# A decoder layer on one core: the stretch from the last output tiles to the feed-forward operands with four engines' instructions in a written order

## The chip, the cores and the metric

One core of a Trainium2 chip runs the whole kernel. Its matmul engine (TensorE, PE in the rows, with PEld for its weight loads), VectorE (DVE), ScalarE (ACT) and GpSimd (POOL) each take instructions from a queue of their own, in order; transfers between memory and the chip are issued on SyncE's queue (SP). The metric is the device time of one execution in microseconds (us), lower is better; the kernel before takes 1395.91 us.

## The reference

One decoder layer on 1024 tokens of width 1024, in float32:

```
h    = rms_norm(x, norm_mix);  proj = h @ w_in
mix  = concat(sparse_attention(proj), gated_recurrence(proj))     # 512 + 512 columns
x    = x + mix @ w_out
h    = rms_norm(x, norm_ffn)                                      # x * rsqrt(mean(x*x) + eps) * norm_ffn
gate, up = split(h @ w_gate_up)                                   # 2816 columns each
x    = x + (silu(gate) * up) @ w_down
```

The change lies where `x + mix @ w_out` and its norm turn into the operands of `h @ w_gate_up`.

## The kernel before

A float32 product is made of three matmuls in a faster format: each factor is split into a high half (an ACT copy that rounds, L111) and a low half (a DVE subtraction, L112), and `mm3` (L117 to L120) adds high x high, high x low and low x high. So the third matmul of each group of three needs the low half of the weights. `product` (L710) splits one weight tile of 128x512 into a tile `wop` and runs `mm3` four times: twelve matmuls of 512 columns.

Tokens come in eight tiles of 128. Attention runs tile by tile; when a tile is done, `nsa_out(t, n)` (L733) multiplies its mixed values with half n of the output weights, adds the result to `x1[:, t]` (L497), and after n = 1 stores the row block to memory (L738) and forms the second norm: an ACT square with a running sum (L242), a reciprocal root on 128x1 numbers by twelve small DVE steps (`rsqrt`, L122 to L131), a scaling on ACT (L745) and the gain `g_bc` on POOL (L746); the tiles from 4 on also have tile t-4 subtracted from their first half (L748). The last tile (t = 7) takes gain and root in one DVE instruction (L743) from a gain page loaded late, `g_last`.

The feed-forward product uses a Strassen-like scheme with 2x2 blocks, so its operands are blocks of `x1` and of sums and differences of them. `operand(op, src, t, bank)` (L720) makes one block of an operand: four PE transposes into a PSUM bank (L724; the tag "s" has four banks), an ACT copy of the high half (L727) and a DVE subtraction for the low half (L728). `b11` is made during attention. The others are b21 and t2o (in `opA`, which takes the place of attention's probabilities `pbig`), b22 and t1o (in `opB`), t3o and t4o (in `opC`): 24 blocks. `pair_a(t)` makes b22 and t1o of tile t+4; `pair_d(t)` makes three differences of tiles t and t+4 on POOL (L987 to L989, the first on DVE for t = 3); `pair_b(t)` makes t2o, t3o and t4o from them. `gate_up_a(f)` loads the weights of feed-forward tile f in four parts and runs its products with b11 and b21. For f = 0 and 1 the b11 products (`first`) have weights loaded into the free `qtok` pages and run at the end of attention. `gate_up_s1` forms weight sums on POOL (L972, L973), from which the first product on opB takes its weights.

What sets the order: the kernel's text gives a priority, and a planner with a model of instruction times orders each engine's queue ahead of the run; waits between engines are semaphores. Tiles with one tag share its buffers in turn (`rpage`: three pages of 128x1024). Pools that end give their memory to the next one; attention's pools `at` (with `g_bc` and the weight tiles) and `gpool` (with `qtok`) lie where `ff` (with `opC`, the differences "d" in six buffers, and the weight pages `epage`) comes later. The PSUM pool "pairs" of attention has to end before "banks" begins (`single_banks`).

Of the kernel before, what the change touches and what calls it, by code (L numbers as in the profile page):

```python
# [8 lines left out]
F32 = mybir.dt.float32  # L9
# [39 lines left out]
def hybrid_layer(ctx: ExitStack, tc: tile.TileContext, x, x_t, par, w_in, k_norm, pos_k, pos_v,  # L49
# [87 lines left out]
    V.tensor_copy(identb, ident)  # L137
    par_t = const.tile([P, 18], F32, name="par_t")
# [97 lines left out]
    def split_of(f):  # L236
        return lambda i: parts_of(f(i))

# [471 lines left out]

    def product(src, op, w=None, o=None):
        o = bank8() if o is None else o
        w = wring.tile([P, 2, 512], F32R, name="wop", tag="w") if w is None else w
        split(w[:, 0], w[:, 1], src)
        for c in range(4):
            sl = slice(c * P, (c + 1) * P)
            mm3(o, w[:, 0, sl], w[:, 1, sl], op[:, 0, c], op[:, 1, c], c == 0, c == 3)
        return o
# [11 lines left out]
    with tc.tile_pool(name="at", bufs=1) as at:  # L730
        g_bc = at.tile([P, D], F32, name="g_bc")
        nc.sync.dma_start(g_bc, norm_ffn[0:1, :].broadcast_to([P, D]))
        def nsa_out(t, n):  # L733
            if n == 0:
                mixed[t] = mix_parts(qtok[:, t].rearrange("p (c n) -> p c n", c=4))
            out_tile(w_t, t, n, *mixed[t], bank_f)
            if n == 1:
                nc.sync.dma_start(x1_d[t * P:(t + 1) * P, :], x1[:, t, :])  # L738
                rs2 = norm_stats(x1[:, t, :], rpage())
                if t == NT - 1:  # L740
                    g_last = rpage()
                    nc.sync.dma_start(g_last, norm_ffn[0:1, :].broadcast_to([P, D]))
                    V.scalar_tensor_tensor(x1[:, t, :], x1[:, t, :], rs2, g_last, op0=OP.mult, op1=OP.mult)  # L743
                    return
# [153 lines left out]
        for i, u in enumerate(units + [None]):  # L898
# [34 lines left out]
            if i == len(units) - NFIRST:  # L933

                for f in range(2):
                    gu_load(qtok[:, f], FS[f], 0, 0)
        first = [product(qtok[:, f], b11, at.tile([P, 2, 512], F32R, name="wop0", tag="q", bufs=3), ps_t())
                 for f in range(2)]
        for t in nq:
            nsa_out(*t)  # L940
    p12.close()
# [3 lines left out]
    single_banks()  # L945
    opA = big.tile([P, 2, 2, 4, 512], F32R, name="opA", tag="A2")
# [3 lines left out]
    b21, t2o, b22, t1o, t3o, t4o = (opA[:, 0], opA[:, 1], opB[:, 0], opB[:, 1], opC[:, 0], opC[:, 1])  # L950
# [3 lines left out]
    def gate_up_a(f):  # L954

        a = {}
        for j in range(2):
# [4 lines left out]
        return a, first.pop(0) if first else product(a[0, 0], b11), product(a[0, 1], b21, o=acc() if f < 2 else None)  # L962
# [15 lines left out]
    def pair_a(t):  # L978
        operand(b22, x1[:, t + 4, 512:1024], t, bank_s)
        if t == 3:  # L980
            V.tensor_tensor(x1[:, 7, 0:512], x1[:, 7, 0:512], x1[:, 3, 0:512], op=OP.subtract)
        operand(t1o, x1[:, t + 4, 0:512], t, bank_s)

    def pair_d(t):
        xa, xb = x1[:, t, :], x1[:, t + 4, :]
        d = dif[t] = [ff.tile([P, 512], F32, name=f"d{i}", tag="d", bufs=6) for i in range(3)]
        (G if t < 3 else V).tensor_tensor(d[0], xb[:, 512:1024], xb[:, 0:512], op=OP.subtract)  # L987
        G.tensor_tensor(d[1], d[0], xa[:, 0:512], op=OP.subtract)
        G.tensor_tensor(d[2], xa[:, 512:1024], d[0], op=OP.subtract)  # L989

    def pair_b(t):
        for i, op in enumerate((t2o, t3o, t4o)):
            operand(op, dif[t][i], t, bank_s)

    for t in range(4):
        operand(b21, x1[:, t, 512:1024], t, bank_s)
    nxt = [gate_up_a(0), gate_up_a(1)]
    for t in range(3):
        pair_a(t)
    for t in range(3):  # L1000
        pair_d(t)
        pair_b(t)
    s1s = [gate_up_s1(0, nxt[0][0])]
    pair_a(3)
    pair_d(3)
    pair_b(3)
    tmp = big.tile([P, 16, 512], F32, name="tmp", tag="A1")
# [290 lines left out]
```

## Time and profile before

| | us |
|---|---|
| three runs | 1395.39, 1395.91, 1396.53 |
| median | 1395.91 |
| the profiled execution | 1396.95 |
| its span, first to last instruction | 1395.2 |
| mean granted clock of TensorE | 0.997 of full speed |

The profiled execution is one more run, and all rows below are from it. Times in the rows count from the start of its span. Busy times of PE contain the latency of its pipeline: matmuls overlap, so what a matmul costs is the distance of two starts. An engine's idle time in square brackets is that before the instruction, with what ended it.

### The profile page before, as it was taken

How to read it: one execution, taken by the hardware profiler on the slowest of the kernel's cores; microseconds unless marked ns; L12 is line 12 of the kernel's file. 1: busy time of each engine (PE TensorE's matmuls, PEld its weight loads, DVE VectorE, ACT ScalarE, POOL GpSimd, SP SyncE). 2: the span in 40 equal slices, each digit the busy share in tenths (PEclk: the TensorE clock that was granted, in tenths of full speed). 3: DMA queues.
4: the chain of work that ended last, by engine and by line, in shares of the span. 5: the costliest groups of instructions: out<-in, count | busy, mean ns of one | idle time of the engine just before them, and what ended most of it. 6: DMA issues, size and time to landing. Idle time of an engine off the chain costs nothing.

```text
span 1395.2 us, 19645 instructions
## 1 busy us (share of the span) xinstructions
PE 1366.1 (98%) x7092; PEld 1127.8 (81%) x7092; DVE 1034.3 (74%) x1937; ACT 596.7 (43%) x1153; POOL 322.2 (23%) x297
## 2 busy tenths in 40 slices
PE   9999999999999999999998999999999999999998
PEld 7888888989977777777776788888888888888887
DVE  5317888626688887888867888888888887578764
ACT  7323333323446666566664433333333333444432
POOL 0001111011035443344345533323323320000000
PEclk9999999999999999999999999999999999999999
DMA  8411110111220001000003233333233336998521
GB/s 326 128 46 31 31 31 29 54 31 46 76 106 1 1 1 61 31 16 16 31 17 106 70 112 99 113 114 113 92 113 98 114 98 234 335 327 317 180 94 53
DMA packets 108768, 135.71 MB, mean 97 GB/s; under 512 B 6112, under 2 KB 63872, under 8 KB 108672
## 3 DMA queue, kind: packets, MB, share of 16 engines
q1 hardware_dynamic: 108672, 134.46, 28.6%
q8 instruction: 56, 0.92, 0.3%
q14 instruction: 40, 0.33, 0.1%
HBM read 105.87 MB, written 28.57 MB: 96 GB/s over the span
## 4 chain that ended last, share of the span: by engine, by line
PE 85%; DVE 10%; ACT 2%; issue 1%; POOL 1%; DMA 0%; ACTq 0%; POOLq 0%; DVEq 0%
PE bank L118 9%; PE bank L119 9%; PE bank L120 9%; PE a L118 8%; PE a L120 8%; PE a L119 8%; PE ps_t L120 4%; PE ps_t L119 4%; PE ps_t L118 4%; PE ps_t L861 3%; PE a L865 2%; PE a L866 2%; PE ps_t L375 1%; PE ps_s L839 1%; DVE nm L847 1%
## 5 line engine op out<-in xcount | busy, mean ns | idle before, releaser
L111 ACT ACTIVATE wop<-rpage 128x512 fp32r<-128x512 f32 x132 | 82.7, 630 | 156.8 <-PE bank L120 70.6
L850 POOL TENSOR_SCALAR pbig<-pbig,den,gates 128x640 f32<-128x640 f32 (+7 forms) x128 | 104.0, 817 | 167.0 <-DVE den L849 147.0
L112 DVE TENSOR_TENSOR wop<-rpage,wop 128x512 fp32r<-128x512 f32 x132 | 101.4, 771 | 13.4 <-ACT wop L111 11.3
L864 DVE TENSOR_TENSOR ph<-ps_t,ph 128x512 fp32r<-128x512 f32 x126 | 84.4, 684 | 18.5 <-ACT ph L863 17.6
L863 ACT ACTIVATE ph<-ps_t 128x512 fp32r<-128x512 f32 x126 | 72.7, 595 | 49.6 <-PE ps_t L861 38.7
L861 PE MATMUL ps_t<-ident,pbig 128*128 128x128 f32 x504 | 78.7, 275 | 2.1 <-POOL pbig L850 2.1
L381 POOL TENSOR_TENSOR kp<-kp,fp 128x256 f32<-128x256 f32 x28 | 20.3, 726 | 231.8 <-PE bank L358 180.3
L861 PEld LDWEIGHTS ps_t<-ident,pbig 128*128 128x128 f32 x504 | 61.0, 141 | 11.9 <-POOL pbig L850 3.2
L112 DVE TENSOR_TENSOR wlo<-wraw,whi 128x1024 fp32r<-128x1024 f32 (+2 forms) x27 | 32.0, 1188 | 46.2 <-PE a L120 19.3
L848 ACT ACTIVATE pbig<-ps_s,nm 128x640 f32<-128x640 f32 (+3 forms) x64 | 55.9, 875 | 24.1 <-DVE nm L847 19.0
L118 PE MATMUL bank<-wop 128*128 128x512 f32 x165 | 64.2, 389 | 0.0
L119 PE MATMUL bank<-wop 128*128 128x512 f32 x165 | 64.2, 389 | 0.0
L120 PE MATMUL bank<-wop 128*128 128x512 f32 x165 | 64.2, 389 | 0.0
L1012 POOL TENSOR_TENSOR tmp<-tmp,rpage 128x512 f32<-128x512 f32 x21 | 31.2, 1488 | 139.2 <-DVE wop L112 139.2
L111 ACT ACTIVATE wop<-act_a 128x512 fp32r<-128x512 f32 x48 | 30.3, 631 | 73.8 <-PE bank L120 48.3
L847 DVE TENSOR_REDUCE nm<-ps_s 128x1 f32<-128x640 f32 (+3 forms) x64 | 58.1, 914 | 4.7 <-PE ps_s L842 3.0
L865 PE MATMUL a<-ph,kv 128*128 128x512 f32 x132 | 58.8, 446 | 2.3 <-ACT ph L863 1.6
L866 PE MATMUL a<-ph,kv 128*128 128x512 f32 x132 | 57.5, 435 | 2.9 <-DVE ph L864 2.4
L112 DVE TENSOR_TENSOR wop<-tmp,wop 128x512 fp32r<-128x512 f32 x42 | 43.7, 1039 | 20.6 <-ACT wop L111 19.7
L111 ACT ACTIVATE wop<-tmp 128x512 fp32r<-128x512 f32 x42 | 26.6, 634 | 70.1 <-POOL tmp L1012 37.5
L112 DVE TENSOR_TENSOR wop<-act_a,wop 128x512 fp32r<-128x512 f32 x48 | 33.2, 691 | 30.7 <-ACT wop L111 30.6
L118 PE MATMUL a<-whi,hT_h 128*128 128x256 f32 (+2 forms) x168 | 55.2, 328 | 0.0
(458 smaller groups left out, 4352.3 us busy)
## 6 DMA issues: line engine op xcount, KB each, us to landing
rpage<-in_w_gate_up_dram SPq DMA_DIRECT2D x86, 256.0 KB, 3.1
raws<-in_w_down_dram SPq DMA_DIRECT2D x35, 512.0 KB, 7.5
act_a<-act_d SPq DMA_DIRECT2D x12, 1024.0 KB, 6.1
act_d<-as SPq DMA_DIRECT2D x33, 256.0 KB, 2.2
act_e<-act_d SPq DMA_DIRECT2D x6, 1024.0 KB, 8.2
act_d<-tmp SPq DMA_DIRECT2D x22, 256.0 KB, 2.2
act_d<-th SPq DMA_DIRECT2D x22, 256.0 KB, 2.1
xn<-in_x_dram SPq DMA_DIRECT2D x8, 512.0 KB, 6.0
```

The lines of the kernel that those rows point to most:

```text
L111: A.activation(hi, src, AF.Copy)
L112: V.tensor_tensor(lo, src, hi.bitcast(F32), op=OP.subtract)
L118: PE.matmul(o, ah, bh, start=first, stop=False, skip_group_check=chained)
L119: PE.matmul(o, ah, bl, start=False, stop=False, skip_group_check=chained)
L120: PE.matmul(o, al, bh, start=False, stop=last, skip_group_check=chained)
L847: V.tensor_reduce(nm, sv, axis=AX.XY, op=OP.max, negate=True)
L850: G.tensor_scalar(pp, pp, den, gates[:, qb, h * 3 + 1 + b:h * 3 + 2 + b], op0=OP.mult, op1=OP.mult)
L861: PE.transpose(pt[:, r * P:(r + 1) * P], wts[r][:, c0:c0 + P], ident)
L863: A.activation(ph[:, 0], pt, AF.Copy)
L864: V.tensor_tensor(ph[:, 1], pt, ph[:, 0].bitcast(F32), op=OP.subtract)
L865: PE.matmul(o, vst[b][:, kb, g, :], ph[:, 0], start=b == 0 and kb == kb0, stop=False)
L866: PE.matmul(o, vst[b][:, kb, g, :], ph[:, 1], start=False, stop=False)
```

## The change

All four engines get a block written by hand (`tc.manual_schedule`): from `hand.enter_context` to `hand.close()` each of PE, DVE, ACT and POOL keeps these instructions in the order of the text. Instructions outside the block may still be placed between them by the planner. SP is not in it.

In the block: the output tile (6, 1), then the b11 product of f = 0, two blocks of b21, output tile (7, 0), b21 of tile 2, output tile (7, 1) in a second PSUM bank (`a0`), b21 and b22 blocks, the b11 product of f = 1, and so on as written. Its weights for f = 1 are split into the place of t2o's high half (`w_first = t2o[:, 0, 0:2]`), which t2o takes over later. The reciprocal roots of tiles 6 and 7 are now a power: `norm_power` leaves mean and epsilon to one DVE step and raises to -0.5 on POOL with a constant `mhalf`. Tile 6 takes its gain from `g_last`, no longer from `g_bc`, and on POOL behind the first differences. The loads of f = 0 bring the second half (j = 1) first. `single_banks` and `opA` come inside attention's pool, ahead of its end. The b21 products of f = 0 and 1 (`second`) stand behind `pair_b(0)` and `pair_b(1)`.

```
--- before.py
+++ after.py
@@ -135,6 +135,8 @@
     make_identity(nc, ident)
     identb = const.tile([P, P], BF16, name="identb")
     V.tensor_copy(identb, ident)
+    mhalf = const.tile([P, 1], F32, name="mhalf")
+    V.memset(mhalf, -0.5)
     par_t = const.tile([P, 18], F32, name="par_t")
     gains = const.tile([P, 24], F32, name="gains")
     lb_a = const.tile([P, 4], F32, name="lb_a")
@@ -235,6 +237,18 @@
 
     def split_of(f):
         return lambda i: parts_of(f(i))
+
+    def norm_power(src, junk):
+
+        ss = small.tile([P, 1], F32, name="n_ss", tag="n_ss")
+        rs = small.tile([P, 1], F32, name="n_rs", tag="n_rs", bufs=NT)
+        A.activation(junk, src, AF.Square, accum_out=ss)
+        V.tensor_scalar(ss, ss, 1.0 / D, EPS, op0=OP.mult, op1=OP.add)
+
+        def power():
+            G.tensor_tensor(rs, ss, mhalf, op=OP.pow)
+            return rs
+        return power
 
     def norm_stats(src, junk):
         ss = small.tile([P, 1], F32, name="n_ss", tag="n_ss")
@@ -708,10 +722,15 @@
         nc.sync.dma_start(dst.rearrange("p (c n) -> p c n", c=4),
                           w_gu3[:, 4 * j:4 * j + 4, k * D_FF + f * P:k * D_FF + (f + 1) * P])
 
+    hand = ExitStack()
+
     def product(src, op, w=None, o=None):
         o = bank8() if o is None else o
         w = wring.tile([P, 2, 512], F32R, name="wop", tag="w") if w is None else w
         split(w[:, 0], w[:, 1], src)
+        return times(w, op, o)
+
+    def times(w, op, o):
         for c in range(4):
             sl = slice(c * P, (c + 1) * P)
             mm3(o, w[:, 0, sl], w[:, 1, sl], op[:, 0, c], op[:, 1, c], c == 0, c == 3)
@@ -730,18 +749,15 @@
     with tc.tile_pool(name="at", bufs=1) as at:
         g_bc = at.tile([P, D], F32, name="g_bc")
         nc.sync.dma_start(g_bc, norm_ffn[0:1, :].broadcast_to([P, D]))
-        def nsa_out(t, n):
-            if n == 0:
+        def nsa_out(t, n, bank=bank_f):
+            if n == 0 and t < NT - 1:
                 mixed[t] = mix_parts(qtok[:, t].rearrange("p (c n) -> p c n", c=4))
-            out_tile(w_t, t, n, *mixed[t], bank_f)
+            out_tile(w_t, t, n, *mixed[t], bank)
             if n == 1:
                 nc.sync.dma_start(x1_d[t * P:(t + 1) * P, :], x1[:, t, :])
+                if t >= NT - 2:
+                    return
                 rs2 = norm_stats(x1[:, t, :], rpage())
-                if t == NT - 1:
-                    g_last = rpage()
-                    nc.sync.dma_start(g_last, norm_ffn[0:1, :].broadcast_to([P, D]))
-                    V.scalar_tensor_tensor(x1[:, t, :], x1[:, t, :], rs2, g_last, op0=OP.mult, op1=OP.mult)
-                    return
                 A.activation(x1[:, t, :], x1[:, t, :], AF.Copy, scale=rs2)
                 G.tensor_tensor(x1[:, t, :], x1[:, t, :], g_bc, op=OP.mult)
                 if t >= 4:
@@ -934,32 +950,48 @@
 
                 for f in range(2):
                     gu_load(qtok[:, f], FS[f], 0, 0)
-        first = [product(qtok[:, f], b11, at.tile([P, 2, 512], F32R, name="wop0", tag="q", bufs=3), ps_t())
-                 for f in range(2)]
-        for t in nq:
+        hand.enter_context(tc.manual_schedule(engines={mybir.EngineType.PE, mybir.EngineType.DVE,
+                                                       mybir.EngineType.Activation, mybir.EngineType.Pool}))
+        w_first = at.tile([P, 2, 512], F32R, name="wop0", tag="q", bufs=3)
+        split(w_first[:, 0], w_first[:, 1], qtok[:, 0])
+        for t in nq[:-2]:
             nsa_out(*t)
+        power = norm_power(x1[:, NT - 2, :], rpage())
+        rs6 = power()
+        first = [times(w_first, b11, ps_t())]
+        mixed[NT - 1] = mix_parts(qtok[:, NT - 1].rearrange("p (c n) -> p c n", c=4))
+        single_banks()
+        opA = big.tile([P, 2, 2, 4, 512], F32R, name="opA", tag="A2")
+        b21, t2o = opA[:, 0], opA[:, 1]
+
+        w_first = t2o[:, 0, 0:2]
+        split(w_first[:, 0], w_first[:, 1], qtok[:, 1])
+        A.activation(x1[:, NT - 2, :], x1[:, NT - 2, :], AF.Copy, scale=rs6)
     p12.close()
 
 
 
-    single_banks()
-    opA = big.tile([P, 2, 2, 4, 512], F32R, name="opA", tag="A2")
     opB = big.tile([P, 2, 2, 4, 512], F32R, name="opB", tag="KV")
     ff = ctx.enter_context(tc.tile_pool(name="ff", bufs=1))
     opC = ff.tile([P, 2, 2, 4, 512], F32R, name="opC", tag="opC")
-    b21, t2o, b22, t1o, t3o, t4o = (opA[:, 0], opA[:, 1], opB[:, 0], opB[:, 1], opC[:, 0], opC[:, 1])
+    b22, t1o, t3o, t4o = (opB[:, 0], opB[:, 1], opC[:, 0], opC[:, 1])
     def epage():
         return ff.tile([P, 512], F32, name="epage", tag="e", bufs=2)
 
-    def gate_up_a(f):
+    def gate_up_load(f, order=(0, 1)):
 
         a = {}
-        for j in range(2):
+        for j in order:
             r = rpage() if f * j != 1 else None
             for k in range(2):
                 a[k, j] = r[:, 512 * k:512 * (k + 1)] if r is not None else epage()
                 gu_load(a[k, j], FS[f], j, k)
-        return a, first.pop(0) if first else product(a[0, 0], b11), product(a[0, 1], b21, o=acc() if f < 2 else None)
+        return a
+
+    def gate_up_a(f):
+
+        a = gate_up_load(f)
+        return a, product(a[0, 0], b11), product(a[0, 1], b21)
 
     def gate_up_sum(f, o1, o2):
         p1, c11 = (tmp[:, 4 * (f % 2) + i] for i in range(2))
@@ -977,33 +1009,56 @@
 
     def pair_a(t):
         operand(b22, x1[:, t + 4, 512:1024], t, bank_s)
-        if t == 3:
-            V.tensor_tensor(x1[:, 7, 0:512], x1[:, 7, 0:512], x1[:, 3, 0:512], op=OP.subtract)
         operand(t1o, x1[:, t + 4, 0:512], t, bank_s)
 
-    def pair_d(t):
+    def pair_d(t, some=(0, 1, 2)):
         xa, xb = x1[:, t, :], x1[:, t + 4, :]
-        d = dif[t] = [ff.tile([P, 512], F32, name=f"d{i}", tag="d", bufs=6) for i in range(3)]
-        (G if t < 3 else V).tensor_tensor(d[0], xb[:, 512:1024], xb[:, 0:512], op=OP.subtract)
-        G.tensor_tensor(d[1], d[0], xa[:, 0:512], op=OP.subtract)
-        G.tensor_tensor(d[2], xa[:, 512:1024], d[0], op=OP.subtract)
-
-    def pair_b(t):
-        for i, op in enumerate((t2o, t3o, t4o)):
-            operand(op, dif[t][i], t, bank_s)
-
-    for t in range(4):
-        operand(b21, x1[:, t, 512:1024], t, bank_s)
-    nxt = [gate_up_a(0), gate_up_a(1)]
-    for t in range(3):
-        pair_a(t)
-    for t in range(3):
-        pair_d(t)
-        pair_b(t)
-    s1s = [gate_up_s1(0, nxt[0][0])]
+        for i in some:
+            d = ff.tile([P, 512], F32, name=f"d{i}", tag="d", bufs=6)
+            dif[t, i] = d
+            (G if t < 3 or i else V).tensor_tensor(d, *((xb[:, 512:1024], xb[:, 0:512]), (dif[t, 0], xa[:, 0:512]),
+                                                       (xa[:, 512:1024], dif[t, 0]))[i], op=OP.subtract)
+
+    def pair_b(t, some=(0, 1, 2)):
+        for i in some:
+            operand((t2o, t3o, t4o)[i], dif[t, i], t, bank_s)
+
+    g_last = rpage()
+    nc.sync.dma_start(g_last, norm_ffn[0:1, :].broadcast_to([P, D]))
+    aw = [gate_up_load(0, (1, 0))]
+    pair_d(0)
+    G.tensor_tensor(x1[:, NT - 2, :], x1[:, NT - 2, :], g_last, op=OP.mult)
+    G.tensor_tensor(x1[:, NT - 2, 0:512], x1[:, NT - 2, 0:512], x1[:, 2, 0:512], op=OP.subtract)
+    operand(b21, x1[:, 0, 512:1024], 0, bank_s)
+    operand(b21, x1[:, 1, 512:1024], 1, bank_s)
+    nsa_out(*nq[-2])
+    operand(b21, x1[:, 2, 512:1024], 2, bank_s)
+    nsa_out(*nq[-1], lambda: ps.tile([P, 512], F32, name="a0", tag="a0", bufs=1))
+    aw.append(gate_up_load(1))
+    operand(b21, x1[:, 3, 512:1024], 3, bank_s)
+    power = norm_power(x1[:, NT - 1, :].rearrange("p (c n) -> p c n", c=2), opC[:, 0, 0, 0:2])
+    operand(b22, x1[:, 4, 512:1024], 0, bank_s)
+    rs7 = power()
+    first.append(times(w_first, b11, ps_t()))
+    operand(t1o, x1[:, 4, 0:512], 0, bank_s)
+    pair_d(1)
+    V.scalar_tensor_tensor(x1[:, NT - 1, :], x1[:, NT - 1, :], rs7, g_last, op0=OP.mult, op1=OP.mult)
+    pair_b(0)
+    second = {0: product(aw[0][0, 1], b21, o=acc())}
+    pair_a(1)
+    pair_d(2)
+    V.tensor_tensor(x1[:, 7, 0:512], x1[:, 7, 0:512], x1[:, 3, 0:512], op=OP.subtract)
+    pair_d(3, (0,))
+    pair_b(1)
+    second[1] = product(aw[1][0, 1], b21, o=acc())
+    pair_a(2)
     pair_a(3)
-    pair_d(3)
+    pair_b(2)
+    pair_d(3, (1, 2))
+    s1s = [gate_up_s1(0, aw[0])]
     pair_b(3)
+    hand.close()
+    nxt = [(aw[f], first[f], second[f]) for f in range(2)]
     tmp = big.tile([P, 16, 512], F32, name="tmp", tag="A1")
 
     def gate_up_b(f, a, s1):
```

## Rows read from the trace of the kernel before

**Rows 1.** The page, part 1: busy us, share of the span, instructions.
```profile
PE 1366.1 (98%) x7092; PEld 1127.8 (81%) x7092; DVE 1034.3 (74%) x1937; ACT 596.7 (43%) x1153; POOL 322.2 (23%) x297
```

**Rows 2.** Stretches: us, busy of PE, PEld, DVE, ACT, POOL, clock, DMA share, GB/s.
```profile
735.63:748.87 13.24, 13.24 (x64) 10.62 (x63) 6.76 (x22) 4.62 (x9) 6.14 (x4) 1.00 0.24 80
748.87:773.68 24.81, 18.26 (x113) 13.62 (x112) 22.75 (x39) 14.37 (x27) 17.50 (x15) 1.00 0.37 106
773.68:800.00 26.32, 26.32 (x119) 21.80 (x118) 23.64 (x35) 11.90 (x22) 10.99 (x8) 1.00 0.29 86
```

**Rows 3.** PE's groups, 748.87 to 773.68: line, output<-input, count | busy, mean ns | idle.
```profile
L724 PE MATMUL bank<-ident,d 128*128 128x128 f32 x48 | 7.2, 279 | 3.2 <-POOL d L988 1.1 <-DVE opB L728 0.7 <-DVE opA L728 0.7
L724 PE MATMUL bank<-ident,x 128*128 128x128 f32 x40 | 5.7, 278 | 2.2 <-DVE opA L728 1.1 <-DVE n_rs L131 0.6 <-DVE opB L728 0.4
```

**Rows 4.** PE in order of time: start us, us, line, output<-input, count, [idle before].
```profile
735.63 0.40 PE L118 MATMUL ps_t<-b,wop 128*128 128x512 f32 x1
...
739.51 0.40 PE L118 MATMUL ps_t<-b,wop 128*128 128x512 f32 x1
...
742.31 0.39 PE L118 MATMUL a<-whi,rpage 128*128 128x512 f32 x1
...
745.07 1.03 PE L724 MATMUL bank<-ident,x 128*128 128x128 f32 x8
...
748.87 1.91 PE L724 MATMUL bank<-ident,x 128*128 128x128 f32 x16
...
761.88 0.50 PE L120 MATMUL a<-opA,wop 128*128 128x512 f32 x1 [0.84 <-DVE wop L112]
...
773.68 0.48 PE L118 MATMUL bank<-opB,wop 128*128 128x512 f32 x1
```

**Rows 5.** DVE's groups of x1[7]'s reciprocal root, 751 to 761.2.
```profile
L131 DVE SCALAR_TENSOR_TENSOR n_rs<-rs_t,n_rs 128x1 f32<-128x1 f32 x3 | 1.7, 570 | 0.0
L130 DVE SCALAR_TENSOR_TENSOR rs_t<-rs_t,rs_v 128x1 f32<-128x1 f32 x3 | 1.6, 518 | 0.0
L129 DVE TENSOR_TENSOR rs_t<-n_rs 128x1 f32<-128x1 f32 x3 | 1.5, 500 | 0.0
```

**Rows 6.** DVE in order of time, inside the stretch.
```profile
752.26 0.53 DVE L129 TENSOR_TENSOR rs_t<-n_rs 128x1 f32<-128x1 f32 x1
...
761.75 2.30 DVE L743 SCALAR_TENSOR_TENSOR x<-x,n_rs,rpage 128x1024 f32<-128x1024 f32 x1
763.97 0.68 DVE L112 TENSOR_TENSOR wop<-epage,wop 128x512 fp32r<-128x512 f32 x1
764.58 0.68 DVE L728 TENSOR_TENSOR opC<-bank,opC 128x512 fp32r<-128x512 f32 x1
```

**Rows 7.** POOL in order of time.
```profile
742.57 2.41 POOL L746 TENSOR_TENSOR x<-x,g_bc 128x1024 f32<-128x1024 f32 x1 [16.73 <-ACT x L745]
...
751.51 1.27 POOL L988 TENSOR_TENSOR d<-d,x 128x512 f32<-128x512 f32 x1
...
761.29 1.69 POOL L973 TENSOR_TENSOR rpage<-rpage 128x512 f32<-128x512 f32 x1
```

**Rows 8.** POOL's groups by shape, whole span: its smallest arithmetic.
```profile
L850 POOL TENSOR_SCALAR pbig<-pbig,den,gates 128x128 f32<-128x128 f32 x16 | 7.8, 492 | 9.0 <-DVE den L849 9.0
```

**Rows 9.** SP's queue in order of time: the first loads into `ff`.
```profile
745.01 0.93 SPq L708 DMA_DIRECT2D epage<-in_w_gate_up_dram  x2
```

**Rows 10.** DVE in order of time, at attention's end.
```profile
740.30 0.69 DVE L511 TENSOR_TENSOR rpage<-qtok,rpage 128x512 fp32r<-128x512 f32 x1
```

**Rows 11.** ACT in order of time: one operand copy.
```profile
749.50 0.60 ACT L727 ACTIVATE opA<-bank 128x512 fp32r<-128x512 f32 x1 [2.65 <-PE bank L724]
```

**Rows 12.** Stretches around clock changes; columns as in rows 2.
```profile
558.00:560.00 2.00, 1.12 (x6) 0.74 (x5) 1.36 (x3) 1.63 (x4) 0.47 (x1) 1.00 0.00 0
560.60:564.00 3.40, 3.40 (x12) 2.61 (x13) 3.40 (x7) 0.99 (x2) 1.95 (x2) 0.52 0.00 0
...
753.00:755.00 2.00, 0.98 (x8) 0.68 (x7) 2.00 (x5) 1.28 (x3) 1.01 (x1) 1.00 0.84 207
```

## The prediction

> **What bounds the kernel now.** I read the page's busy shares first: the matmul engine (PE) is busy 98% of the span [rows 1], so what can be won or lost is PE's idle time, stage by stage. Then the table by stretches around the change [rows 2]. Before 748.87 us and behind 773.68 us PE runs through; between them, in 24.81 us, it has 113 instructions, 88 of them transposes [rows 3] and all but one of the others 512-column matmuls, while VectorE (DVE) is busy 22.75 us. "Busy" contains pipeline latency (18.26 us of it here), so I price PE by its cadence [rows 4]: 12 matmuls go from 742.31 to 745.07, 2.76 us for a product of twelve and 0.23 for one; 16 transposes took 1.91 us and 8 took 1.03, so eight more cost 0.88, 0.44 us for the four of one operand block. 22 blocks (9.7 us) and 24 matmuls (5.5 us) are 15.2 us of work, so **9.6 us are idle**. That is all the change can win here. One row shows the kind of wait (0.84 us before 761.88, until DVE had written a weight's low half); the stage ends when the products on opB start at 773.68.
>
> DVE's groups show why it is late [rows 5]: the reciprocal root of x1[7] takes 4.8 us in nine steps on 128x1 numbers, 0.50 to 0.57 us each. The step at 752.26 lasted 0.53 us and ended at 752.79 [rows 6], when the GpSimd (POOL) subtraction begun at 751.51 ended (752.78) [rows 7]. The gain of x1[7] took 2.30 us at 761.75 and ended 1.07 us behind the POOL operation that ran to 762.98. So a DVE instruction with two SBUF inputs waits for a running POOL instruction, at most its 1.27 us. An operand block costs DVE 0.61 us (763.97 to 764.58), and as it reads PSUM it does not wait.
>
> **The change part by part.** In the block written by hand each of PE, ScalarE (ACT), DVE and POOL takes its instructions in the written order; I follow the four queues with these durations.
>
> Removed: the reciprocal roots of x1[6] and x1[7], 24 small DVE steps; the second one's were 5 us of DVE in the stretch. In place of each stand one small DVE step and one power on POOL. No row shows a power. Its nearest rows are POOL's smallest arithmetic here, 0.49 us [rows 8], and its longest, the 2.41 us gain; I take 0.5 to 1. For x1[7] it is then ready at about 750.5, and its reader, the gain on DVE, stands behind an operand block until 752.4: both ends cost nothing while that block waits for PE, and beyond 3 us each us counts. For x1[6] ACT's scaling waits for the power, and the copies of two b21 blocks queue behind it on ACT; their cover is PE's product of 2.76 us. The new -0.5 constant is one small DVE step at the start, when nothing waits for it.
>
> Given back: x1[6]'s gain moves from g_bc to a page that is loaded later, so attention's pool closes without it. In the trace before, the first load into the pool that follows it was issued at 745.01 [rows 9], when POOL's gain on g_bc ended (742.57 + 2.41). Now that can be at about 741.5, and the first differences on POOL start 4 to 5 us earlier. SP's loads move forward with it: the gain page and tile 0's second half go out near 740, their first readers are at 745 and 752. I cost them at zero, since what waits for the gain page is POOL's x1[6], read 10 us and more later. The store of x1[7] is passed by loads only.
>
> Step A, to the last output tile. Attention's operand for x1[7] was ready at 740.99 (740.30 + 0.69) [rows 10], with small root steps between; now about 740.95. PE does the first product from 735.63 to 739.51 among attention's last matmuls, two b21 blocks to 740.4, waits 0.55, then 2.76 + 0.44 + 2.76: the last output tile ends at **746.9**. Before it ended at 748.87 with one product more (2.76) and one block less (0.44) done, so this is 0.35 us late, not early.
>
> Step B. Two blocks, the second product, four blocks: PE is at 747.8, 750.55 and **752.3**. Then comes the b21 product of tile 0, whose third matmul needs the low half of its weight. On DVE that split stands behind the t1o block (transposed by 751.0, ACT 0.60 [rows 11], DVE done at 752.4), x1[7]'s gain (1.07) and three blocks (1.83), and takes 0.68 itself: 756.0 without POOL. Gain and split have two SBUF inputs and POOL works through differences all the time; each waits 0 to 1.27 us, I take half, so 757.3. PE idles from 752.3 to 757.3 but for two matmuls: **4.5 us** (3.2 to 5.7).
>
> Step C. PE's other ten matmuls end at 759.6; the next block reaches DVE through transposes and ACT at 760.9. DVE has idled since the split and now does seven 512-column instructions (4.3) and the next split (0.64 + 0.68): 766.6. PE has done its five blocks by 762.1 and idles to 766.6 but for two matmuls: **4.1 us**.
>
> Step D. Ten matmuls to 768.9, DVE from 770.2 with ten blocks (6.1) to 776.2. Four PSUM banks let PE run about three blocks ahead, so its last transposes end at 774.6. The opB product then needs a weight whose low half DVE makes either ahead of the last blocks (start 774.6, +0.9 us against 773.68) or behind them (776.2 + 0.68 - 0.46 = 776.4, +2.7).
>
> Sum: +0.9 to +2.7 us. PE's idle time is not removed but changes place, because twice PE waits for DVE and then DVE for PE. The hand block comes first in the text, so I lean to the upper end: **+2.2 us**. If no POOL instruction is ever in the way it is about -1; if always, +5. The profiled execution lasted 1396.95 us (span 1395.2 and 1.75 around it), 1.04 above the median of the runs, 1395.91. On its own time the sum gives 1399.15, on the median **1398.1**.
>
> **The rivals.** (1) Slower: the clock falls. Behind a stretch of attention that ends at 560, with PE busy 1.12 of 2 us, the granted clock was 0.52 for 3.40 us [rows 12], nearly all at 1.2 GHz instead of 2.4. The stretch 753 to 755, busy 0.98 of 2 us, kept 1.00. The new idle stretches are 4 to 5 us each with two matmuls in them, emptier than either. Ten matmuls at half rate cost 2.3 us more, 0.9 if only part of them, and DVE waits for them: with both stretches +1.8 to +4.6 on top, 1400 to 1402.7, middle 1401. It decides as soon as a fall overlaps a product. The Trainium skill ("TensorE: Matmul & The Clock Gate", section "HAM oscillation — how this bites in real kernels") says that an array left waiting between bursts is throttled and starts the next one slow; by that rule this rival holds in both places, and of the two rows one speaks for it and one against.
> (2) Faster: the splits don't wait. From 746.9 DVE has some 16 us of work; were both low halves made ahead of the blocks that stand before them, step B would lose 1.9 us less and step C 4.2: -3.9, 1392. Against it: the split is written behind, on a queue that keeps the order.
> (3) The block changes little, as the planner had found nearly that order: 1396 within 1.
>
> **How the numbers follow.** Chances: forecast 0.46, clock 0.31, faster 0.13, little 0.10. A measurement of this kernel tells about 0.2% (2.8 us) from no change. Faster 0.13. Slower: the clock, and a quarter of the forecast's case (its upper end with POOL in the way), 0.31 + 0.11 = 0.42. Same 0.45. The range goes from the faster rival's value, 1392, to the clock's upper end, 1402.6; the forecast's own is 1395 to 1401.
>
> **What would show it.** Right: between 747 and 777 two PE waits of 3 to 5 us that end on a split's subtraction, each followed by a DVE wait of over 3 us; no root steps there; first differences on POOL near 742. The clock rival: a granted clock near 0.5 right behind one of these waits. Wrong: PE idle under 7 us between 747 and the products on opB, their start before 772, or a power of over 3 us.

## The result and the profile after

The changed kernel takes **1404.95 us** in the median of 4 runs (1404.0 to 1406.63), the kernel before 1396.01 beside it: ratio 1.0066, 95% interval 1.0048 to 1.0083, 9 us slower. That is 2.35 us above the upper end of the forecast's range. The profiled execution lasted 1406.63 us with a span of 1404.8, 9.6 more than the span of before (1395.2). PE's work is the same, its busy time is not:

The page of the kernel after, part 1 (as [rows 1]):
```profile
PE 1371.9 (98%) x7092; PEld 1131.8 (81%) x7092; DVE 1033.6 (74%) x1916; ACT 596.8 (42%) x1153; POOL 324.2 (23%) x299
```

The same 7092 matmuls take 5.8 us longer than in [rows 1], so something made matmuls slow; DVE has 21 instructions fewer. PE in order of time shows where (start us, us, line, output<-input, count, idle before and what ended it), against [rows 4]:
```profile
746.83 1.03 PE L743 MATMUL bank<-ident,x 128*128 128x128 f32 x8
...
753.73 0.50 PE L118 MATMUL a<-opA,wop 128*128 128x512 f32 x1 [1.36 <-ACT wop L111]
754.06 0.40 PE L119 MATMUL a<-opA,wop 128*128 128x512 f32 x1
756.79 0.80 PE L120 MATMUL a<-opA,wop 128*128 128x512 f32 x1 [2.33 <-DVE wop L112]
757.38 0.63 PE L118 MATMUL a<-opA,wop 128*128 128x512 f32 x1
...
761.22 1.39 PE L743 MATMUL bank<-ident,x 128*128 128x128 f32 x8
762.45 1.04 PE L743 MATMUL bank<-ident,d 128*128 128x128 f32 x8
...
765.51 0.50 PE L118 MATMUL a<-opA,wop 128*128 128x512 f32 x1 [1.21 <-ACT wop L111]
...
768.80 0.80 PE L120 MATMUL a<-opA,wop 128*128 128x512 f32 x1 [2.56 <-DVE wop L112]
...
772.76 1.91 PE L743 MATMUL bank<-ident,x 128*128 128x128 f32 x16
774.87 3.67 PE L743 MATMUL bank<-ident,d 128*128 128x128 f32 x24 [0.20 <-DVE opB L747]
779.95 0.50 PE L118 MATMUL bank<-opB,wop 128*128 128x512 f32 x1 [1.41 <-ACT wop L111]
...
782.18 0.61 PE L120 MATMUL bank<-opB,wop 128*128 128x512 f32 x1 [1.50 <-DVE wop L112]
...
786.16 0.39 PE L118 MATMUL bank<-opA,wop 128*128 128x512 f32 x1
```

Read it from below. In the kernel before, the product that began at 773.68 was done 12 matmuls later, when the next one began:
```profile
776.52 0.39 PE L118 MATMUL bank<-opA,wop 128*128 128x512 f32 x1
```

Now it is done at 786.16: 9.64 us late, the whole difference of the spans. Nothing is lost or won behind it. Three products, itself the last, have the same picture: a wait of 1.2 to 1.4 us for ACT's high half, two matmuls, a wait of 1.5 to 2.6 us for DVE's low half, and then matmuls that follow one another at 0.43 us (757.38 to 761.22, nine of them) where [rows 4] has 0.23.

The stretches behind each wait give the reason (us, busy of PE, PEld, DVE, ACT, POOL, granted clock, DMA share, GB/s):
```profile
755.20:762.00 6.80, 5.21 (x14) 4.18 (x15) 1.53 (x2) 0.00 (x0) 3.82 (x3) 0.50 0.25 73
762.00:768.80 6.80, 2.84 (x20) 1.96 (x19) 5.77 (x8) 3.18 (x6) 2.50 (x2) 1.00 0.00 0
768.80:772.20 3.40, 3.40 (x8) 2.75 (x9) 0.00 (x0) 0.00 (x0) 0.00 (x0) 0.50 0.00 0
...
782.50:785.90 3.40, 3.40 (x9) 2.64 (x8) 3.25 (x3) 1.99 (x4) 2.97 (x2) 0.51 0.02 5
```

The clock is granted at 0.50, so 1.2 GHz instead of 2.4, three times, each time at a wait or right behind it, and each time most of the ten matmuls left of a product fall into it. In the second stretch, in which PE is emptiest (2.84 of 6.80 us), the clock is back at full: of the transposes between the first two products only the first eight (1.23 us) still pay. The fall comes with the wait and is paid by the product.

DVE shows the other half of the waiting (as [rows 6]):
```profile
755.54 1.20 DVE L112 TENSOR_TENSOR wop<-rpage,wop 128x512 fp32r<-128x512 f32 x1
762.84 1.29 DVE L747 TENSOR_TENSOR opB<-bank,opB 128x512 fp32r<-128x512 f32 x2 [6.11 <-ACT opB L746]
...
767.27 1.48 DVE L112 TENSOR_TENSOR wop<-epage,wop 128x512 fp32r<-128x512 f32 x1
774.03 2.48 DVE L747 TENSOR_TENSOR opB<-bank,opB 128x512 fp32r<-128x512 f32 x4 [5.29 <-ACT opB L746]
...
780.24 1.28 DVE L999 TENSOR_TENSOR tmp<-a,tmp 128x512 f32<-128x512 f32 x2
781.44 0.68 DVE L112 TENSOR_TENSOR wop<-s,wop 128x512 fp32r<-128x512 f32 x1
```

Behind each split DVE stands idle, 6.11 and 5.29 us, until PE has done a slow product and the next transposes. In front of the third split stand two sums into tmp, 1.20 us. On POOL, the power costs 0.56 us and is done 2.2 us before its reader, the gain on DVE, starts at 752.34 behind an operand block; the first difference starts at 741.98:
```profile
741.98 1.30 POOL L1019 TENSOR_TENSOR d<-x 128x512 f32<-128x512 f32 x1 [7.94 <-ACT opA L746]
...
749.58 0.56 POOL L249 TENSOR_TENSOR n_rs<-n_ss,mhalf 128x1 f32<-128x1 f32 x1
```

### The profile page after: what moved, and what is told of

It reads as the page before. It is cut to its first block, busy times and chain, and to the rows that moved or that the text cites. A ratio compares the mean times of both kernels' runs of the same rounds, so it can differ in the third digit from the quotient of the medians.

```text
span 1404.8 us, 19629 instructions
## 1 busy us (share of the span) xinstructions
PE 1371.9 (98%) x7092; PEld 1131.8 (81%) x7092; DVE 1033.6 (74%) x1916; ACT 596.8 (42%) x1153; POOL 324.2 (23%) x299
## 4 chain that ended last, share of the span: by engine, by line
PE 85%; DVE 9%; ACT 3%; issue 1%; POOL 1%; DMA 0%; ACTq 0%; POOLq 0%; DVEq 0%
PE bank L120 9%; PE bank L118 9%; PE bank L119 9%; PE a L120 8%; PE a L118 8%; PE a L119 8%; PE ps_t L118 4%; PE ps_t L120 4%; PE ps_t L119 4%; PE ps_t L877 3%; PE a L881 2%; PE a L882 2%; PE ps_t L389 1%; PE ps_s L855 1%; PE ps_s L856 1%
## 5 line engine op out<-in xcount | busy, mean ns | idle before, releaser
L120 PE MATMUL a<-whi,hT_l 128*128 128x256 f32 (+2 forms) x168 | 55.0, 327 | 0.0
```

What stands on the lines that cost most here:

```text
L120: PE.matmul(o, al, bh, start=False, stop=last, skip_group_check=chained)
```

## The experiments

The first theory is the prediction's mechanism with its rival made the larger part: the splits of three weights stand behind operand blocks on DVE (two of them in the written block, that of the opB product outside it, where the planner placed it), PE and DVE wait for each other in turn, and the clock falls come from these waits. The other theories: it is the clock alone; it is DVE's whole work; it is another part of the change (power, buffers, moved loads). Every time below stands beside runs of the kernel before on the same chip (1396.81 us for the first four experiments, 1396.45 for the next four, 1396.23 for the last four; the changed kernel's 1404.95 stands beside 1396.01).

**e1_early: both b21 splits written earlier.** Same instructions, two splits moved on DVE and ACT.
```diff
+    w_s0 = wring.tile([P, 2, 512], F32R, name="wop", tag="w")
+    split(w_s0[:, 0], w_s0[:, 1], aw[0][0, 1])
     operand(t1o, x1[:, 4, 0:512], 0, bank_s)
...
-    second = {0: product(aw[0][0, 1], b21, o=acc())}
+    second = {0: times(w_s0, b21, acc())}
+    w_s1 = wring.tile([P, 2, 512], F32R, name="wop", tag="w")
+    split(w_s1[:, 0], w_s1[:, 1], aw[1][0, 1])
     pair_a(1)
...
-    second[1] = product(aw[1][0, 1], b21, o=acc())
+    second[1] = times(w_s1, b21, acc())
```


> The changed kernel with one edit: the splits of the two b21 weights stand earlier in the hand order, tile 0's ahead of the first t1o block, tile 1's ahead of pair_a(1), so that PE finds both low halves made. Theory 1 (PE waits for the split that stands behind DVE's blocks, and DVE then for PE; the clock falls in those waits): PE goes from the pair_b(0) transposes into the product without a wait, the two waits of 2.3 to 2.6 us before a third matmul vanish, the clock stays at 1.00 but perhaps at the opB product, and the opB products start near 769.5 instead of 779.95: 1391 to 1394 us, faster than the kernel before by 2 to 5 us. Theory 2 (the block's other parts cost the time: the power on POOL, differences moved forward that hold the port, buffers given back): the splits matter little, 1402 to 1405.

Measured: 1394.71 us (1393.91 to 1397.19), ratio to before 0.999, interval 0.9981 to 0.9999. Ten us come back by moving two splits; the time is 0.7 above the first theory's range, and by the ratio the gain on the kernel before is 1.4 us, where 2 to 5 were expected. PE in order of time, and one stretch:
```profile
767.84 0.50 PE L118 MATMUL bank<-opB,wop 128*128 128x512 f32 x1 [1.41 <-ACT wop L111]
...
770.07 0.50 PE L120 MATMUL bank<-opB,wop 128*128 128x512 f32 x1 [1.50 <-DVE wop L112]
```
```profile
771.00:774.40 3.40, 3.40 (x10) 2.66 (x9) 3.25 (x3) 2.59 (x5) 2.37 (x2) 0.52 0.00 0
```
Both b21 products run through at full clock; the opB product, whose split was not moved, has the waits that it had after the change (1.41 and 1.50), and behind them the only low clock of this part, 0.52 in 771.0 to 774.4. In these two products the place of the split decides both the wait and the clock.

**e2_fill: PE kept busy in the waits.** 18, 18 and 14 matmuls whose result nobody reads, in front of the three products; nothing else is changed.
```diff
     pair_b(0)
+    accs = [acc(), acc()]
+    for _ in range(18):
+        PE.matmul(accs[1], b11[:, 0, 0, 0:P], b11[:, 0, 1], start=True, stop=True)
-    second = {0: product(aw[0][0, 1], b21, o=acc())}
+    second = {0: product(aw[0][0, 1], b21, o=accs[0])}
...
```


> The changed kernel with 50 idle matmuls added where PE waits (18 ahead of each b21 product, 14 behind the last transposes), 0.23 us each, with results that nobody reads: PE's waits are filled and no other instruction moves. Theory 1a (the clock falls cost about 5.5 us: 2.1 + 1.7 + 1.7 in the three products that ran at 0.5, the waits themselves the rest): the clock stays at 1.00, the three products take 2.8 us each and the time is 1398.5 to 1400.5. Theory 1b (the waits alone cost the time and the half clock is hidden behind DVE): no gain, 1404 to 1406.

Measured: 1402.27 us (1401.15 to 1403.28), ratio 1.0039 (1.0024 to 1.0053), between the ranges of the two theories. The clock stays up, a stretch and PE:
```profile
755.20:762.00 6.80, 6.60 (x38) 5.26 (x37) 3.07 (x5) 2.23 (x5) 3.73 (x3) 1.00 0.23 69
```
```profile
780.58 0.50 PE L118 MATMUL bank<-opA,wop 128*128 128x512 f32 x1
...
782.16 0.50 PE L120 MATMUL bank<-opA,wop 128*128 128x512 f32 x1 [0.84 <-DVE wop L112]
```
The opB product is done at 780.58 and not at 786.16. So of its 9.64 us of delay the clock made 5.6, and 4.1 are waiting as such. Behind that the next product now waits for its own split (0.84 us at 782.16), which in the changed kernel had been ready because the slow product gave DVE time. The span is 4.3 us shorter than that of the profiled execution after the change; the medians are only 2.7 apart, as that execution lies 1.7 above its own median. So part of each theory holds: the clock costs time, and it alone does not explain the loss.

**e3_planner: the same text without the written order.** The line that opens the hand block is taken out.
```diff
-        hand.enter_context(tc.manual_schedule(engines={mybir.EngineType.PE, mybir.EngineType.DVE,
-                                                       mybir.EngineType.Activation, mybir.EngineType.Pool}))
```


> The changed kernel without the hand order: every instruction as in the change, the four engines' order again made by the planner. Theory 1 (the written order makes the waits): the planner fills them, near the kernel before, 1392 to 1397. Theory 2 (the other parts of the change make the loss): 1402 to 1406 remains.

Measured: 1397.16 us (1395.62 to 1399.38), ratio 1.0002 (0.9993 to 1.0011), just above the first theory's range and 7.8 less than the changed kernel. DVE in order of time says why, and PE what is left:
```profile
744.87 1.80 DVE L112 TENSOR_TENSOR wop<-rpage,wop 128x512 fp32r<-128x512 f32 x1
746.60 1.77 DVE L112 TENSOR_TENSOR wop<-epage,wop 128x512 fp32r<-128x512 f32 x1
```
```profile
770.72 0.50 PE L118 MATMUL bank<-opB,wop 128*128 128x512 f32 x1 [1.41 <-ACT wop L111]
...
772.95 0.80 PE L120 MATMUL bank<-opB,wop 128*128 128x512 f32 x1 [1.49 <-DVE wop L112]
```
The planner makes both b21 splits at 745 to 748 us, 10 and 20 us ahead of where the written order has them (755.54 and 767.27). So the power, the buffers and the loads by themselves do not make the loss; the written order does, by where it puts these two splits. The third is another matter: here too the opB product waits 1.41 and 1.49 us, because the planner has its split at 772.21, behind the last operand blocks and two sums, as in the changed kernel. The third product's part of the loss is therefore not the written order's own; it goes when that split is moved too (e6).

**e4_power: the power alone.** The kernel before, with the power for x1[6] and x1[7] and nothing else.
```diff
-                rs2 = norm_stats(x1[:, t, :], rpage())
+                rs2 = norm_power(x1[:, t, :], rpage())() if t >= NT - 2 else norm_stats(x1[:, t, :], rpage())
...
```


> The kernel before with the reciprocal roots of the last two tiles as a power on POOL, and nothing else of the change. The power took 0.56 us in the changed kernel, the root 5 us of DVE in a stretch where DVE had no gap: if DVE sets that stretch, 2 to 4 us less than before, 1392 to 1394; if the power costs (theory 2), 1396 to 1399.

Measured: 1401.01 us (1399.98 to 1401.44), ratio 1.0028 (1.0017 to 1.0039): slower, and above both expected ranges, though DVE has 5 us less to do here. DVE, then PE, then the split in the kernel before:
```profile
754.74 1.84 DVE L757 SCALAR_TENSOR_TENSOR x<-x,n_rs,rpage 128x1024 f32<-128x1024 f32 x1 [0.72 <-DMA rpage<-in_norm_ffn_dram]
...
765.79 1.43 DVE L1001 TENSOR_TENSOR d<-x 128x512 f32<-128x512 f32 x1 [3.33 <-PE bank L738]
...
775.26 0.68 DVE L112 TENSOR_TENSOR wop<-s,wop 128x512 fp32r<-128x512 f32 x1
```
```profile
776.00 0.51 PE L120 MATMUL bank<-opB,wop 128*128 128x512 f32 x1 [3.21 <-DVE wop L112]
```
```profile
766.97 0.68 DVE L112 TENSOR_TENSOR wop<-s,wop 128x512 fp32r<-128x512 f32 x1
```
With the root gone, the gain is there before its page (0.72 us), and the planner's order is another: the opB product's split goes from 766.97, in the kernel before, to 775.26, behind the last operand block. Of the time won on DVE 3.33 us are spent as one idle stretch on DVE. So this run has two changes in it, the power and the planner's new order, and does not price the power by itself. Why the planner chose so was not tried.

**e5_highs: the low half needed later.** The eight matmuls of a product that read its weight's high half first, then the four on the low half; the splits stay where the changed kernel has them.
```diff
         for c in range(4):
             sl = slice(c * P, (c + 1) * P)
-            mm3(o, w[:, 0, sl], w[:, 1, sl], op[:, 0, c], op[:, 1, c], c == 0, c == 3)
+            PE.matmul(o, w[:, 0, sl], op[:, 0, c], start=c == 0, stop=False)
+            PE.matmul(o, w[:, 0, sl], op[:, 1, c], start=False, stop=False)
+        for c in range(4):
+            PE.matmul(o, w[:, 1, c * P:(c + 1) * P], op[:, 0, c], start=False, stop=c == 3)
```


> The changed kernel with one edit in times: the eight matmuls of a product that read the weight's high half first, the four that read its low half behind them, so that the low half is needed 1.4 us later (six matmuls of 0.23 us) in every product. Theory 1 (PE and DVE wait in turn for a split written too late, and the clock's falls come of these waits): the three waits for a split's subtraction, near 756.8, 768.8 and 782.2 us in the changed kernel, are each about 1.4 us shorter, about 4 us less, 1400 to 1401.5; if with 10 matmuls fewer to be done behind each wait one of the falls also goes, 1.5 to 2 us less for each, down to 1396. Theory 2 (the loss is DVE's work alone, PE's waits only show it): within 1 us of the changed kernel's 1404.95.

Measured: 1397.6 us (1396.84 to 1399.08), ratio 1.0007 (0.9997 to 1.0016), 7.4 less than the changed kernel, so the larger of the first theory's two cases. PE, and the whole stage as one stretch, the changed kernel's below it:
```profile
752.51 0.50 PE L736 MATMUL a<-opA,wop 128*128 128x512 f32 x1 [1.35 <-ACT wop L111]
...
755.63 1.19 PE L739 MATMUL a<-opA,wop 128*128 128x512 f32 x4 [1.01 <-DVE wop L112]
...
760.59 0.50 PE L736 MATMUL a<-opA,wop 128*128 128x512 f32 x1 [1.20 <-ACT wop L111]
...
763.91 1.21 PE L739 MATMUL a<-opA,wop 128*128 128x512 f32 x4 [1.21 <-DVE wop L112]
```
```profile
747.00:776.00 29.00, 21.78 (x123) 16.29 (x121) 21.99 (x32) 14.87 (x29) 19.84 (x16) 1.00 0.17 55
```
```profile
747.00:786.16 39.16, 28.33 (x133) 21.78 (x131) 24.91 (x35) 17.85 (x35) 22.62 (x17) 0.83 0.13 41
```
The waits for the low half are 1.01 and 1.21 us instead of 2.33 and 2.56, with eight matmuls in front of them instead of two, and no clock falls. PE's busy share of the stage is the same (21.78 of 29.00 us is 0.75; 28.33 of 39.16 is 0.72), the granted clock is 1.00 against 0.83. At about the same idle share, with shorter waits and more matmuls between them, no clock was lost.

**e6_early_q and e7_q_highs: the opB product's split early too.** e6 is e1 with one more split moved, ahead of the last three operand blocks; e7 is e6 with the order of e5.
```diff
     s1s = [gate_up_s1(0, aw[0])]
+    w_q = wring.tile([P, 2, 512], F32R, name="wop", tag="w")
+    split(w_q[:, 0], w_q[:, 1], s1s[0])
     pair_b(3)
...
-        q = product(s1, t1o)
+        q = product(s1, t1o) if f else times(w_q, t1o, bank8())
```


> The kernel of e1_early, and the weight split of the first opB product too is written into the hand block, ahead of the last three operand blocks (pair_b(3)), and its matmuls taken from it. Theory 1: the two waits of 1.41 and 1.50 us in front of and within that product (767.84 and 770.07 us in e1_early) go, and the clock's fall at 768.8 with them: 2.9 us less, with the fall up to 4.5, so 1390.5 to 1392. Theory 2 (DVE is full from 748 to 772 us in e1_early, so the wait only moves to the next product's split, 772.46 us there): 1394 to 1395.5.

> The kernel of e6_early_q, with the order of e5_highs in its products (high half's eight matmuls first). Theory 1 (what is left are waits for a low half): up to 1.4 us less than e6_early_q, 1390 to 1392. Theory 2 (DVE's whole work sets the stage's end): the same as e6_early_q within 1 us.

Measured: e6 1391.42 us (1390.4 to 1392.15), ratio 0.9958 (0.9944 to 0.9973); e7 1391.24 (1391.09 to 1391.38), ratio 0.9958 (0.9941 to 0.9975). Both beat the changed kernel by 13.5 us and the kernel before by 5. PE of e6:
```profile
768.29 0.50 PE L120 MATMUL bank<-opB,wop 128*128 128x512 f32 x1 [0.19 <-DVE wop L112]
...
771.35 0.50 PE L118 MATMUL bank<-opA,wop 128*128 128x512 f32 x1 [0.51 <-ACT wop L111]
```
Of 1.41 and 1.50 us of waiting 0.19 is left there, the clock is 1.00 throughout, and 0.51 goes to the next product. e7 adds nothing that can be told apart: once the splits are early, the order within a product makes no difference that these runs show.

**e8_root: the root on DVE again, in the good order.** e1 with x1[7]'s reciprocal root in DVE's steps.
```diff
-    power = norm_power(x1[:, NT - 1, :].rearrange("p (c n) -> p c n", c=2), opC[:, 0, 0, 0:2])
+    rs7 = norm_stats(x1[:, NT - 1, :].rearrange("p (c n) -> p c n", c=2), opC[:, 0, 0, 0:2])
...
-    rs7 = power()
```


> The kernel of e1_early, but x1[7]'s reciprocal root is made in DVE's steps again, as before the change, instead of by a power on POOL (x1[6] keeps the power). If DVE bounds the stage once the splits are early: its idle time there is under 1 us from 748 to 770, so the 4.8 us of steps come nearly whole, 1398 to 1400. If DVE's time is not what sets the end: 1394.5 to 1396.

Measured: 1401.37 us (1400.79 to 1402.9), 6.7 more than e1, beyond what was expected. One group of DVE between 748 and 756 us, and PE:
```profile
L129 DVE TENSOR_TENSOR rs_t<-n_rs 128x1 f32<-128x1 f32 x3 | 3.5, 1162 | 0.1
```
```profile
756.02 1.08 PE L743 MATMUL bank<-ident,d 128*128 128x128 f32 x4 [5.22 <-DVE opB L747]
```
Three of the nine steps take 1162 ns each where [rows 5] has 500, and each of the three ends when the POOL subtraction beside it ends (the first at 749.75 and 749.74); DVE is held for 7.2 us (748.00 to 755.19), PE waits 5.22, and the clock is at 0.66 in the mean of 751.8 to 758.6 and again of 772.2 to 779.0 (a fall near the opB product e1 has too). So in this order the power is worth its place; the 6.7 us hold the steps, their waits for POOL and the low clock behind them together.

**e9_power_highs, e10_before_highs: the order within a product, elsewhere.** The edit of e5 put on e4_power and on the kernel before.

> The kernel of e4_power (the kernel before with the power on POOL for x1[6] and x1[7], nothing else), with the order of e5_highs in the products. e4_power was slower than before; its first opB product waits 3.21 us for its weight's low half, which DVE splits at 775.26 us behind all operand blocks, where the kernel before had it at 766.97. Theory 1 (that wait and the clock's fall behind it make e4_power slower): the low half is needed 1.4 us later, so 1.4 us less, with the fall gone up to 3.5: 1397 to 1399.6. Theory 2 (the late gain page and DVE's order of the operand blocks make it, the low half is only next in line): as e4_power within 0.7 us, 1400.3 to 1401.7.

> The kernel before with the order of e5_highs in its products and nothing else: what that order is worth where hardly a product waits. Theory 1 (it is worth what the waits for a low half last): 0.84 and 0.27 us of them stand in the stretch, so about 1 us less than before, 1395 to 1396.5. If the order is worth something in every product of the feed-forward, more than 3 us less: under 1393.5.

Measured: e9 1402.28 us (1401.94 to 1402.48), ratio 1.0043 (1.0028 to 1.0058); e10 1395.79 (1394.19 to 1397.77), ratio 0.9997 (0.9988 to 1.0007). e10 is no change, so the gain of e5 is not a gain of every product. Both ranges for e9 lie below what was measured, and the first theory fell:
```profile
777.98 1.19 PE L734 MATMUL bank<-opB,wop 128*128 128x512 f32 x4 [1.83 <-DVE wop L112]
780.38 0.80 PE L731 MATMUL bank<-opA,wop 128*128 128x512 f32 x1 [1.21 <-ACT wop L111]
```
The wait for the low half is 1.4 us shorter (1.83 instead of 3.21), as it should be, but the next product's split is just as late on ACT and DVE, so PE waits 1.21 there and starts at the low clock. What makes e4_power slow is not that one wait alone: the split behind it is as late.

**e11_q_planner: e6 without the written order** (the edit of e3 on e6).

> The kernel of e6_early_q without the hand-made order: the planner places the same instructions, the three early splits among them. Theory 1 (early splits need the written order, the planner moves them behind operand blocks again): 1395 to 1397.5, as e3_planner. Theory 2 (the place in the text is enough): 1391 to 1392.5.

Measured: 1394.29 us (1392.35 to 1396.03), ratio 0.9984 (0.9974 to 0.9993), between the two ranges. The planner keeps the opB split early, but waits 1.74 us for an operand block at 757.35, and the clock is 0.66 from 757 to 762. Against e3 (1397.16) that is about 3 us less, and of the three splits only the third has another place, as the planner has the b21 splits early in both (744.87 and 746.60 in e3, 745.59 and 747.33 here); the written order is worth another 3.

**e12_gain_first: POOL's order.** e6 with x1[6]'s gain and subtraction written ahead of the first differences.
```diff
-    pair_d(0)
     G.tensor_tensor(x1[:, NT - 2, :], x1[:, NT - 2, :], g_last, op=OP.mult)
     G.tensor_tensor(x1[:, NT - 2, 0:512], x1[:, NT - 2, 0:512], x1[:, 2, 0:512], op=OP.subtract)
+    pair_d(0)
```


> The kernel of e6_early_q, but POOL does x1[6]'s gain and subtraction (2.39 and 1.30 us) ahead of the first three differences and not behind them, so these come 3.7 us later, about where they would be without attention's buffers given back early. If the early differences are what the stage needs: 3 to 4 us more, 1394.5 to 1395.5. If they have room (they end at 746.2 us in e6_early_q and are transposed from about 751): 0 to 1 us more, 1391.4 to 1392.5.

Measured: 1392.52 us (1391.62 to 1393.36), at the upper end of the second range, but the run does not test what it was made for:
```profile
736.77 2.39 POOL L1029 TENSOR_TENSOR x<-x,rpage 128x1024 f32<-128x1024 f32 x1 [3.79 <-DMA rpage<-in_norm_ffn_dram]
...
741.95 1.30 POOL L1019 TENSOR_TENSOR d<-x 128x512 f32<-128x512 f32 x1 [1.37 <-issue]
```
The gain went into POOL's idle time ahead of 742, and the differences start where they did (741.98 after the change, 742.33 in e6), after 1.37 us in which POOL stood idle: the gain's place in the order does not push them back by its 3.7 us. What it does cost stands further up: POOL's subtraction at 739.25 holds up DVE on attention's last operand (1.65 us instead of 0.69), and PE waits 0.95 us for it at 741.19, a wait that e6 does not have. What the early return of attention's buffers is worth was not measured by itself and stays open.

## Why the prediction was wrong

**Step A was right**: forecast 746.9 for the end of the last output tile, measured 746.83.

**Step B was right in place and nearly in size**: forecast 757.3 for the product's third matmul, measured 756.79. PE waited 1.36 and 2.33 us where 4.5 were forecast. The split waited for POOL as assumed (1.20 us instead of 0.68).

**Step C was right but for the clock.** Forecast 766.6, measured 768.80. Behind 756.79 the ten matmuls took 4.43 us (to 761.22) instead of 2.3, and eight transposes 1.23 (to 762.45) instead of 0.88: 2.5 us late, less the 0.5 that step B was early, is 2.0 of the 2.2.

**Step D missed a term of its own.** The ten matmuls from 768.80 to 772.76 cost 1.7 more. And the low half of the opB weight was forecast behind DVE's last blocks at the latest; it stands behind two sums into tmp as well, 1.20 us.

**The sum.** The upper end of step D puts the end of the opB product 2.6 us later than before (start 776.4, third matmul 776.86, ten more 2.29: 779.15 against 776.52). Add the low clock, 2.1 + 0.35 behind the first wait, 1.7 behind the second and 1.7 behind the third (782.18 to 786.16 is 3.98 instead of 2.29), 5.85 in all, and the two sums, 1.2: 9.65, measured 9.64. That it fits to 0.01 is luck: step B was 0.5 early, and about as much was lost in steps C and D in small amounts that the sum leaves out. The other bound is near as well: with the clock held up (e2) 4.1 of it are left, against 2.6 + 1.2.

**The step that failed** is the clock, left out of the sum: the mechanism stands in the text as the first rival, with its place and its sign ("a granted clock near 0.5 right behind one of these waits"), but it was kept out of the sum, with a chance of 0.31, on one row for it and one against [rows 12], although the text itself calls the new idle stretches emptier than either row. And its size was taken for two products, 4.6 us at most; there were three. The third was left out because step D was only asked when the opB product could start, not how PE would wait in front of it and within it. Per product the size was nearly right (2.45 us with the transposes behind it, 1.7 and 1.7, against 0.9 to 2.3). Where the text has 1.8 to 4.6 the runs showed 5.85, and it belonged in the forecast: 2.2 + 5.85 is 1404 us. The smaller term that was missing, 1.2 us, is that of the two sums. (The upper end of the clock rival by its own sum is 1402.7, not the 1402.6 of the range; it changes nothing.) The signs of the forecast all came, the two waits of PE (3.7 and 3.8 us, in two parts each), DVE's of 6.11 and 5.29, no root steps, the first difference at 741.98, and the sign of the clock rival came with them.

What the prediction says of the faster rival was right as a mechanism too: "were both low halves made ahead of the blocks that stand before them", 1392. e1 does that and gives 1394.71; the rival too forgot the third product, which is worth 3.3 us (e6: 1391.42). As a reading of the change as it stands the rival was rightly turned down: the splits are written behind the blocks, on a queue that keeps the order.

The Trainium skill ("TensorE: Matmul & The Clock Gate", section "HAM oscillation — how this bites in real kernels") says that an array left waiting long enough between bursts starts the next burst slow, each time anew. The changed kernel agrees, three times in three (0.50, 0.50, 0.51). In e5 it did not bite: there too PE waits between bursts, 1.0 to 1.4 us at a time, and the clock stays at 1.00.

## What to carry to other kernels

In an order written by hand the weight split of a product belongs ahead of the operand blocks that the product also needs, as soon as it depends on nothing that PE still has to do; written in its natural place, next to its product, it made PE and DVE wait in turns here. What stands outside a written block has to be followed too: the third split stood behind the last blocks and two sums because the planner put it there. A wait can cost twice: the three pairs of waits here lasted 2.9 to 3.8 us, and the product behind each lost another 1.7 to 2.1 us to the half clock. So price a new wait with the half clock in the sum, and do so for every product that follows one. Work taken off an engine is not priced by its length: the same power gave 6.7 us in e8 against e1, and in e4, where the planner's order changed with it, the time rose by 4 us.

## What the runs showed of the hardware

Ahead of each of the three falls in the changed kernel PE did transposes, waited, did two matmuls and waited again (1.36 and 2.33 us, 1.21 and 2.56, 1.41 and 1.50). In e5, whose b21 products have eight matmuls between the two waits (1.35 and 1.01 us, 1.20 and 1.21), the clock stayed at 1.00. Whether the length of the waits or the matmuls between them made the difference, the runs do not separate: e1's opB product, with two matmuls between waits of 1.41 and 1.50 us, hardly longer than those of e5, was granted 0.52.

The same low clock comes and goes further up, in code that no edit touches: 560.6 to 564.0 us has it in the kernel before and after [rows 12], and so does 424.1 to 427.5 (0.52 and 0.51), while e10_before_highs has neither. These are 424.1 to 427.5 and 560.6 to 564.0 of e10, then the first of them of e9:
```profile
424.10:427.50 3.40, 3.40 (x23) 2.96 (x24) 3.36 (x10) 2.37 (x7) 2.59 (x5) 1.00 0.01 2
...
560.60:564.00 3.40, 3.26 (x18) 2.43 (x19) 3.40 (x8) 2.35 (x6) 1.94 (x2) 1.00 0.00 0
```
```profile
424.10:427.50 3.40, 3.40 (x18) 2.97 (x19) 3.25 (x10) 2.29 (x7) 2.61 (x5) 0.61 0.01 2
```
e9 comes to its last output tiles 1.7 us later than e4_power with the same work ahead of them (first sum into x1[7] at 746.26 and 744.54 us). Each of these falls costs up to 1.7 us (3.40 us at about half rate), which would fit single runs of one kernel that lie up to 3.6 us apart (1394.19 to 1397.77 in e10); a difference of 1 us between two medians is not read here.
